# All modulation rows on TensorE, in four column groups of the array, and none left for attention

## The chip, the cores and the metric

The kernel runs on one core of a Trainium2 chip. The core has TensorE (matmuls, shown as PE, its weight loads as PEld), VectorE (DVE), ScalarE (ACT), GpSimd (POOL) and SyncE (SP), which here only issues transfers. Each engine takes its instructions in the order in which they were written for it, and engines wait for each other by semaphores. The metric is the time of one execution on the device, in microseconds (us).

## The reference, cut to what matters

One layer of a diffusion backbone over 512 latent and 256 context tokens of width 1024. The conditioning vector `c` gives six modulation vectors for the latent tokens, and the learned vector `c_ctx` gives those of the context tokens; all that is computed from them here is

```python
mod  = (silu(c) @ w_mod + b_mod).reshape(B, 6, D)        # w_mod: 1024 x 6144
modc = (silu(c_ctx) @ w_mod + b_mod).reshape(6, D)       # only shift and scale 0, 1 are used
h  = modulate(rmsnorm(x, norm_mix), mod[0], mod[1])      # h * (1 + scale) + shift
hc = modulate(rmsnorm(ctx, norm_mix), modc[0], modc[1])
p  = h @ w_in + b_in                                     # q, kv, rope key, Hyena input, gates
attn = attention(q, keys and values of context and latent)
hy   = hyena(...)                                        # long convolutions by FFT
x = x + mod[2] * merge_branches(attn, hy, gates)
h2 = modulate(rmsnorm(x, norm_ffn), mod[3], mod[4])
x = x + mod[5] * moe(h2)                                 # 64 experts, top 8, and a shared one
return rmsnorm(x, final_norm)
```

So `mod` is a product of one vector (two vectors for the first two parts) with a matrix of 1024 x 6144 fp32 numbers, 25 MB.

## The kernel before, in words

The matrix `w_mod` is cut into 24 column blocks of 256; a block is 1024 x 256, that is 8 pieces of the contraction with 128 rows each. Blocks 0 to 7 (shift and scale of the first norm) are needed at once and are computed in the **prologue**, by `mod_rows` (line 196): eight fp32 matmuls per block, with the two columns of `c2` (silu of `c` and of `c_ctx`) as the stationary side and the weight piece `wm` as the moving side, into the PSUM tile `pm`. ScalarE copies the two rows out (`row`), two transposes (`ptm`, line 205) turn them into columns, VectorE adds the bias into `sh`. `sh` feeds `stream`, which makes the modulated, transposed tokens `hT` and `hTc`. While this runs, the Hyena filters (`filt`) use the same engines.

Blocks 8 to 23 are needed only after attention, as rows in the DRAM tensor `modd`. Before the change, twelve of them (`NM = 12`) are computed by `mod_later` (line 481) between the projections of the **Hyena and gate stage** (`conv_block`, `long_conv`, `gate`): SP loads four `wn` tiles of 256 KB per block into three buffers; ScalarE multiplies each piece by its 128 numbers of silu(`c`) (lines 489, 493) and GpSimd adds the pieces up in `ac` (line 494), or, in every third block at first, VectorE does both in one instruction (line 491). One matmul with a column of ones (`pn`, line 498) then sums over the partitions, VectorE adds the bias row `br`, and GpSimd writes the row to `modd`. `br` has one buffer, and the PSUM tag `ms` of `pn` has one bank. The last four blocks are computed in **attention** by `mod_last` (line 792), with GpSimd for products and sums and the tiles `mb0`, `mb1`, and finished by two matmuls `pnl` (line 837).

The program is written stage by stage, but it is not run in that order: a scheduler sets the order of each engine's instructions before the run, from priorities and its own estimates, so that work of a later line can stand ahead of an earlier one. On each engine that order is then fixed. Attention's first matmuls are those of the keys (`pkn`), the values (`pv`) and the queries (`pq`); the gate matmuls are `pg`, and the Hyena inverse transform is `py`, which reads the table `tit`. Nearly all transfers from DRAM are issued by SP, in order, one queue for all of them.

Of the kernel before, what the change touches and what calls it, by code (L numbers as in the profile page):

```python
# [11 lines left out]
F32 = mybir.dt.float32  # L12
# [9 lines left out]
D = 1024  # L22
# [29 lines left out]
def kernel(ctx: ExitStack, tc: tile.TileContext, x, ctxt, wmod, bmod, win, wuq, wuk, wuv, wba, wbh,  # L52
# [73 lines left out]
    def v(col, n=1, p=128):  # L126
        return vec[:p, col:col + n]
# [15 lines left out]

    scb = const.tile([128, 8], F32, name="scb")
    cb2 = const.tile([128, 12], F32, name="cb2")
# [28 lines left out]
    sp.dma_start(w2t, fw2)  # L174
    sc = mp.tile([128, 16], F32, name="sc")
    act.activation(sc, v(V_C, 16), AF.Silu)
    wmt = {}
    order = [0, 4, 1, 5, 2, 6, 3, 7]
    xs = {"l": [], "c": []}

    def mod_load(q):
# [9 lines left out]

    c2 = mp.tile([128, 8, 2], F32, name="c2")
    dve.tensor_copy(c2[:, :, 0], sc[:, 0:8])
    dve.tensor_copy(c2[:, :, 1], sc[:, 8:16])
    sh = mp.tile([128, 16, 2], F32, name="sh")

    def mod_rows(q):
        pm = bank(f"pm{q}", 256, "pm")
        for j in range(8):
            mm(pm[:2], c2[:, j, :], wmt[q][j // 4][:, j % 4, :], j == 0, j == 7)  # L200
        row = mp.tile([2, 256], F32, name=f"row{q}", tag="row")
        act.copy(row, pm[:2])
        pt = bank(f"ptm{q}", 4, "ms")
        for i in range(2):
            pe.transpose(pt[:, 2 * i:2 * i + 2], row[:, i * 128:(i + 1) * 128], ident[:2, :2])
        dve.tensor_tensor(sh[:, 2 * q:2 * q + 2, :], pt.rearrange("p (i c) -> p i c", c=2),
                          v(V_BM + 2 * q, 2).unsqueeze(2).to_broadcast([128, 2, 2]), ALU.add)
# [50 lines left out]
    for q in range(4):  # L258
# [3 lines left out]
        split(w3p[q // 2][:, q % 2, 0], w3p[q // 2][:, q % 2, 1], xq, lo_eng=gp)  # L262
    sp.dma_start(tit, ti)
    rl1 = fp.tile([128, 2, 4], F32, name="rl1")
# [98 lines left out]
    for i, q in enumerate(order):  # L363
        if i >= 2:
            mod_rows(q)
            if i + 3 < 8:
                mod_load(order[i + 3])
        if i % 2 == 1:
            js = slice(i - 1, i + 1)
            dve.tensor_scalar(A[:, js], sh[:, 8 + i - 1:8 + i + 1, :], 1.0, None, ALU.add)  # L370
            dve.tensor_tensor(A[:, js], A[:, js], v(V_NM + i - 1, 2).unsqueeze(2).to_broadcast([128, 2, 2]), ALU.mult)
            for j in range(i - 1, i + 1):
                stream(j, "l", 0, hT)
                stream(j, "c", 1, hTc)
    mst.close()
    p1st.close()
# [101 lines left out]
    m2p = m2.enter_context(tc.tile_pool(name="m2p", bufs=1, reuse_waits="tile"))  # L478
    act.activation(scb, v(V_C, 8), AF.Silu)

    def mod_later(q, on_dve):

        ac = m2p.tile([128, 256], F32, name=f"ac{q}", tag="ac", bufs=2)
        for j in range(8):
            if j % 2 == 0:
                wq = m2p.tile([128, 2, 256], F32, name=f"wn{q}{j}", tag="wn", bufs=3)
                sp.dma_start(wq, wmod[8 + q, :, j:j + 2, :])
            if j == 0:
                act.mul(ac, wq[:, 0], scb[:, j:j + 1])
            elif on_dve:  # L490
                dve.scalar_tensor_tensor(ac, wq[:, j % 2], scb[:, j:j + 1], ac, ALU.mult, ALU.add)
            else:
                act.mul(wq[:, j % 2], wq[:, j % 2], scb[:, j:j + 1])  # L493
                gp.tensor_tensor(ac, ac, wq[:, j % 2], ALU.add)  # L494
        br = m2p.tile([1, 256], F32, name=f"br{q}", tag="br", bufs=1)
        sp.dma_start(br, bmod[:, q * 256:(q + 1) * 256])
        pm = bank(f"pn{q}", 256, "ms")
        mm(pm[:1], ones[:, 0:1], ac)
        dve.tensor_tensor(br, br, pm[:1], ALU.add)
        gp.dma_start(modd[:, q * 256:(q + 1) * 256], br)  # L500

    def conv_block(i):

        ps, = proj(i, f"hy{i}")
        raw = up.tile([128, T], F32, name=f"raw{i}", tag="raw", bufs=2)
        act.activation(raw, ps, AF.Identity, bias=v(V_BIN + i))
        d = up.tile([128, T], F32, name=f"u{i}", tag="u", bufs=12)
        act.activation(d, ps, AF.Identity, bias=cb2[:, i:i + 1], scale=v(V_CW + 12 + i))
        w0, w2 = v(V_CW + i), v(V_CW + 24 + i)
        dve.scalar_tensor_tensor(d[:, 128:512], raw[:, 0:384], w0, d[:, 128:512], ALU.mult, ALU.add)  # L510
        dve.scalar_tensor_tensor(d[:, 1:128], raw[:, 384:511], w0, d[:, 1:128], ALU.mult, ALU.add)
        dve.scalar_tensor_tensor(d[:, 0:384], raw[:, 128:512], w2, d[:, 0:384], ALU.mult, ALU.add)
        dve.scalar_tensor_tensor(d[:, 384:511], raw[:, 1:128], w2, d[:, 384:511], ALU.mult, ALU.add)
        mod_later(chunk[0], chunk[0] % 3 == 2)
        chunk[0] += 1
        return d
# [78 lines left out]
    chunk = [0]  # L595
    NM = 12
    LATE = 5
# [26 lines left out]
    for i in range(16 - LATE):  # L624
        gate(i)
        if chunk[0] < NM:
            mod_later(chunk[0], False)
            chunk[0] += 1
# [85 lines left out]
    xt = [modp.tile([128, D], F32, name=f"xt{a}", tag=f"xt{a}") for a in range(NA)]  # L714
    mb = [modp.tile([128, D], F32, name=f"mb{i}", tag=f"mb{i}") for i in range(2)]
    hyst = ExitStack()
# [74 lines left out]

    def mod_last(i):

        k, j2 = divmod(i, 4)
        ac = mb[1][:, k * 256:(k + 1) * 256]
        wq = mb[0][:, i % 2 * 512:i % 2 * 512 + 512].rearrange("p (j c) -> p j c", j=2)
        tc.keep_in_program_order(sp.dma_start(wq, wmod[8 + NM + k, :, 2 * j2:2 * j2 + 2, :]))
        tc.keep_in_program_order(gp.tensor_tensor(
            wq, wq, scb[:, 2 * j2:2 * j2 + 2].unsqueeze(2).to_broadcast([128, 2, 256]), ALU.mult))
        if j2 == 0:  # L800
            gp.tensor_tensor(ac, wq[:, 0], wq[:, 1], ALU.add)
        else:
            for j in range(2):
                gp.tensor_tensor(ac, ac, wq[:, j], ALU.add)

    for u in range(2 * H + 2):
# [6 lines left out]
        if 7 <= u < 11:  # L813
# [4 lines left out]
            gp.tensor_tensor(hyT[kt][:, 1], raw, hyT[kt][:, 0].bitcast(F32), ALU.subtract)  # L818
        if 2 <= u < 10:
            mod_last(2 * u - 4)  # L820
            mod_last(2 * u - 3)
        if u % 2 == 0 and u // 2 + 1 < H:
# [7 lines left out]
        if u >= 2:  # L830
            mix(u - 2)
    row = mb[0][0:1]
    sp.dma_start(row, bmod[:, NM * 256:])
    for n in range(2):
        cs = slice(n * 512, (n + 1) * 512)
        pm = bank(f"pnl{n}", tag="pq")
        mm(pm[:1], ones[:, 0:1], mb[1][:, cs])
        dve.tensor_tensor(row[:, cs], row[:, cs], pm[:1], ALU.add)
    gp.dma_start(modd[:, NM * 256:], row)
    ast.close()  # L840
# [700 lines left out]
```

## Time and profile before

| | |
|---|---|
| time, median of 3 runs | 1391.62 us (1391.15 to 1392.55) |
| the profiled execution's own time | 1393.19 us |
| its span | 1391.4 us |
| TensorE busy | 1285.2 us, 92% of the span |
| VectorE, ScalarE, GpSimd busy | 1143.1, 902.6, 427.0 us |
| granted TensorE clock, mean | 0.972 of 2.4 GHz |
| data moved | 332.79 MB |

The span is what the hardware profiler saw of the one profiled execution, from its first to its last instruction; the execution's own time is 1.8 us longer. Busy times of different engines overlap. A matmul is pipelined, so the sum of single durations is more than the time that TensorE was busy; shares are of the union. Every fp32 matmul appears as two instructions. The mixture of experts takes the time from about 600 us to the end, and the change has no instruction in it.

### The profile page before, as it was taken

Reading aid. Unit: us, or ns where it says so; the run is one execution under the profiler, and the core shown is the slowest. Engines: PE = TensorE matmul, PEld = TensorE weight load, DVE = VectorE, ACT = ScalarE, POOL = GpSimd, SP = SyncE. Lnnn points to the kernel's source line nnn. Section 1 sums busy time; section 2 is a strip of 40 time slices with the busy share of each in tenths; the row PEclk is TensorE's granted clock in tenths of the full one; section 3 lists DMA queues with packets and bytes.
Section 4 is the critical chain, followed back from the end, with each engine's and each line's share of the span. In section 5 each row is a group of like instructions: output and inputs, shape, how many; then the busy total and the mean of one; then the engine's idle time right before and its main releaser. Section 6 shows DMA issues by size and latency. Waiting matters only on the chain.

```text
span 1391.4 us, 19516 instructions
## 1 busy us (share of the span) xinstructions
PE 1285.2 (92%) x6758; PEld 1045.1 (75%) x6758; DVE 1143.1 (82%) x1735; ACT 902.6 (65%) x1366; POOL 427.0 (31%) x341
## 2 busy tenths in 40 slices
PE   6999998887999998899999999999999999999970
PEld 2476886666888786778888888888888888888750
DVE  5879899788788647778988988889888888889855
ACT  4556553443777436546787877778788787777851
POOL 2433146756576256441112111211111111111120
PEclk8999999998999999999999999999999999999995
DMA  9444345454233556467999999899999999999944
GB/s 330 172 137 147 113 153 168 158 172 155 87 105 102 187 170 224 164 268 269 324 319 330 319 317 316 275 325 314 318 323 312 322 327 333 296 313 293 320 111 179
DMA packets 83875, 332.79 MB, mean 239 GB/s; under 512 B 14433, under 2 KB 15981, under 8 KB 56383
## 3 DMA queue, kind: packets, MB, share of 16 engines
q1 hardware_dynamic: 70366, 305.19, 61.3%
q0 software_dynamic: 11104, 22.14, 8.3%
q10 hardware_dynamic: 2304, 4.20, 0.8%
q8 instruction: 53, 0.87, 0.2%
q14 instruction: 48, 0.39, 0.1%
HBM read 296.91 MB, written 52.97 MB: 251 GB/s over the span
## 4 chain that ended last, share of the span: by engine, by line
PE 68%; DVE 10%; DMA 10%; issue 5%; POOL 3%; ACT 3%; SPq 0%; POOLq 0%; DVEq 0%; ACTq 0%
PE pge L100 8%; PE pge L99 8%; PE pge L101 8%; PE pxe L1158 4%; PE pxe L1159 4%; PE pye L101 4%; PE pye L99 4%; PE pye L100 4%; DMA accd<-Ye,ixe 4%; DMA wn<-in_wmod_dram 3%; POOL ac L494 2%; DMA accd<-Ys,ixs 1%; PE phy L101 1%; PE phy L99 1%; PE phy L100 1%
## 5 line engine op out<-in xcount | busy, mean ns | idle before, releaser
L1019 POOL DMA_INDIRECT accd<-Ye,ixe x64 | 111.8, 1747 | 601.2 <-ACT Ye L1018 306.6
L1158 PE MATMUL pxe<-oge,h2h 128*128 128x256 f32 x512 | 131.2, 289 | 0.3
L1159 PE MATMUL pxe<-oge,h2l 128*128 128x256 f32 x512 | 126.9, 280 | 0.0
L1158 PEld LDWEIGHTS pxe<-oge,h2h 128*128 128x128 f32 x512 | 96.4, 188 | 3.7 <-issue 0.6
L1159 PEld LDWEIGHTS pxe<-oge,h2l 128*128 128x128 f32 x512 | 96.4, 188 | 3.1
L494 POOL TENSOR_TENSOR ac<-ac,wn 128x256 f32<-128x256 f32 x56 | 67.0, 1196 | 46.8 <-ACT wn L493 32.3
L1018 ACT COPY Ye<-pye 128x1024 f32<-128x1024 f32 x64 | 65.0, 1016 | 7.6 <-PE pye L101 6.1
L991 ACT ACTIVATE aae<-pge 128x256 f32<-128x256 f32 x64 | 24.7, 386 | 32.5 <-PE pge L101 32.5
L493 ACT ACTIVATE wn<-wn,scb 128x256 f32<-128x256 f32 x56 | 25.6, 501 | 30.6 <-DMA wn<-in_wmod_dram 29.8
L92 PE MATMUL pm<-wm,c 128*2 128x256 f32 x128 | 35.1, 428 | 0.8 <-DMA wm<-in_wmod_dram 0.8
L753 PE MATMUL pT<-ident,P 128*128 128x128 f32 x192 | 31.2, 277 | 4.9 <-DVE PT41l L106 1.5
L1139 DVE TENSOR_TENSOR oge<-iot,posm 128x256 fp32r<-128x256 f32 x64 | 23.7, 418 | 13.2 <-PE pxe L1159 13.2
L732 DVE TENSOR_REDUCE st<-S 128x1 f32<-128x768 f32 x32 | 30.3, 948 | 1.3 <-PE S L101 1.1
L992 DVE SCALAR_TENSOR_TENSOR aae<-aae,wge,pge 128x256 f32<-128x256 f32 x64 | 30.5, 476 | 0.7
L734 ACT ACTIVATE P<-S,st 128x768 f32<-128x768 f32 x32 | 29.1, 910 | 1.8 <-DVE st L732 1.4
L293 POOL TENSOR_TENSOR ab<-ab,f 128x256 f32<-128x256 f32 x12 | 10.7, 892 | 61.8 <-DVE f L292 35.9
L753 PEld LDWEIGHTS pT<-ident,P 128*128 128x128 f32 x192 | 21.9, 140 | 9.2 <-DVE PT41l L106 1.8
L92 PEld LDWEIGHTS pm<-wm,c 128*2 128x2 f32 x128 | 10.8, 92 | 20.9 <-issue 10.1
L92 PEld LDWEIGHTS sle<-R,oge 128*64 128x64 f32 x256 | 23.1, 137 | 4.2
L95 PE MATMUL pte<-ident,aae 128*128 128x128 f32 x128 | 24.4, 272 | 0.0
L92 PE MATMUL sle<-R,oge 128*64 128x4 f32 x256 | 23.1, 189 | 0.0
L95 PEld LDWEIGHTS pte<-ident,aae 128*128 128x128 f32 x128 | 17.6, 140 | 7.3
(7025 smaller groups left out, 4955.2 us busy)
## 6 DMA issues: line engine op xcount, KB each, us to landing
gu0e<-in_wgu_dram SPq DMA_DIRECT2D x64, 1024.0 KB, 7.4
gu1e<-in_wgu_dram SPq DMA_DIRECT2D x64, 1024.0 KB, 7.2
de<-in_wd_dram SPq DMA_DIRECT2D x64, 1024.0 KB, 6.8
wn<-in_wmod_dram SPq DMA_DIRECT2D x48, 256.0 KB, 3.2
wm<-in_wmod_dram SPq DMA_DIRECT2D x16, 512.0 KB, 8.0
rg<-in_win_dram SPq DMA_DIRECT2D x32, 256.0 KB, 2.9
rwo<-in_wout_dram SPq DMA_DIRECT2D x32, 256.0 KB, 3.1
rhy<-in_win_dram SPq DMA_DIRECT2D x24, 256.0 KB, 2.9
```

Of the source, the lines that this page charges most:

```text
L92: pin(pe.matmul(o, lhsT, rhs, start=start, stop=stop))
L95: pin(pe.transpose(o, i, idn))
L99: pe.matmul(o, lt[0], rt[0], start=start, stop=False)
L100: pe.matmul(o, lt[0], rt[1], start=False, stop=False)
L101: pe.matmul(o, lt[1], rt[0], start=False, stop=stop)
L494: gp.tensor_tensor(ac, ac, wq[:, j % 2], ALU.add)
L753: pe.transpose(pT[:, i * 128:(i + 1) * 128], P[:, kt * 128:(kt + 1) * 128], ident)
L992: dve.scalar_tensor_tensor(self.aa, self.aa, self.wg, pg[:, FF:], ALU.mult, ALU.mult)
L1018: act.copy(Y, py)
L1019: gp.indirect_dma_start(out=accd, out_offset=bass.IndirectOffsetOnAxis(ap=self.ix, axis=0), in_=Y, in_offset=None, compute_op=ALU.add, bou ...
L1158: pe.matmul(o, h2h[:, a, js], oh, start=(a % 2 == 0), stop=False)
L1159: pe.matmul(o, h2l[a][:, js], oh, start=False, stop=(a % 2 == 1))
```

## The change

All 24 blocks go to TensorE. `mod_parts` puts the eight pieces of a block's contraction in turn into four column groups of the array: piece j goes to output partitions 32 (j mod 4) and up, with a stationary side `sc32` of 32 columns, of which the first holds silu(`c`), the second silu(`c_ctx`) and the rest zeros. The output tile then holds four partial sums in partitions 0, 32, 64 and 96. One more matmul per row or turn with `cols32` (ones at those four partitions) adds the four up. `mod_later` now makes all of blocks 8 to 23 (`NM = 16`), and `mod_last`, `pnl`, the tiles `mb` and the sums on ScalarE, GpSimd and VectorE are gone. In the prologue the copied-out rows are put in `tit`, whose own load moves behind the last of them.

```diff
-    scb = const.tile([128, 8], F32, name="scb")
+    sc32 = const.tile([128, 8, 32], F32, name="sc32")
+    gp.memset(sc32, 0.0)
+    cols32 = const.tile([128, 32], F32, name="cols32")
+    dve.tensor_reduce(cols32, ident.rearrange("p (g c) -> p c g", g=4), AX.X, ALU.add)
...
-    sc = mp.tile([128, 16], F32, name="sc")
-    act.activation(sc, v(V_C, 16), AF.Silu)
+    for i in range(2):
+        act.activation(sc32[:, :, i], v(V_C + 8 * i, 8), AF.Silu)
...
+    def mod_parts(pm, w):
+
+
+        for j in range(8):
+            g = 32 * (j % 4)
+            mm(pm[g:g + 32], sc32[:, j], w(j), j < 4, j >= 4)
...
     def mod_rows(q):
         pm = bank(f"pm{q}", 256, "pm")
-        for j in range(8):
-            mm(pm[:2], c2[:, j, :], wmt[q][j // 4][:, j % 4, :], j == 0, j == 7)
-        row = mp.tile([2, 256], F32, name=f"row{q}", tag="row")
-        act.copy(row, pm[:2])
+        mod_parts(pm, lambda j: wmt[q][j // 4][:, j % 4, :])
+
+        row = tit[:, q % 4].rearrange("p r c -> p (r c)")
+        act.copy(row, pm)
         pt = bank(f"ptm{q}", 4, "ms")
         for i in range(2):
-            pe.transpose(pt[:, 2 * i:2 * i + 2], row[:, i * 128:(i + 1) * 128], ident[:2, :2])
+            mm(pt[:, 2 * i:2 * i + 2], row[:, i * 128:(i + 1) * 128], cols32[:, 0:2])
...
-    sp.dma_start(tit, ti)
     rl1 = fp.tile([128, 2, 4], F32, name="rl1")
...
                 stream(j, "c", 1, hTc)
+    sp.dma_start(tit, ti)
...
-    def mod_later(q, on_dve):
-
-        ac = m2p.tile([128, 256], F32, name=f"ac{q}", tag="ac", bufs=2)
-        for j in range(8):
-            if j % 2 == 0:
-                wq = m2p.tile([128, 2, 256], F32, name=f"wn{q}{j}", tag="wn", bufs=3)
-                sp.dma_start(wq, wmod[8 + q, :, j:j + 2, :])
-            if j == 0:
-                act.mul(ac, wq[:, 0], scb[:, j:j + 1])
-            elif on_dve:
-                dve.scalar_tensor_tensor(ac, wq[:, j % 2], scb[:, j:j + 1], ac, ALU.mult, ALU.add)
-            else:
-                act.mul(wq[:, j % 2], wq[:, j % 2], scb[:, j:j + 1])
-                gp.tensor_tensor(ac, ac, wq[:, j % 2], ALU.add)
+    def mod_later(q):
+
+        wq = []
+        for h in range(4):
+            wq.append(m2p.tile([128, 2, 256], F32, name=f"wn{q}{h}", tag="wn", bufs=3))
+            sp.dma_start(wq[h], wmod[8 + q, :, 2 * h:2 * h + 2, :])
         br = m2p.tile([1, 256], F32, name=f"br{q}", tag="br", bufs=1)
         sp.dma_start(br, bmod[:, q * 256:(q + 1) * 256])
-        pm = bank(f"pn{q}", 256, "ms")
-        mm(pm[:1], ones[:, 0:1], ac)
-        dve.tensor_tensor(br, br, pm[:1], ALU.add)
+        pm = bank(f"pn{q}", tag="ms")
+        mod_parts(pm[:, 0:256], lambda j: wq[j // 2][:, j % 2])
+        ac = m2p.tile([128, 256], F32, name=f"ac{q}", tag="ac")
+        act.copy(ac, pm[:, 0:256])
+        mm(pm[:1, 256:512], cols32[:, 0:1], ac)
+        dve.tensor_tensor(br, br, pm[:1, 256:512], ALU.add)
         gp.dma_start(modd[:, q * 256:(q + 1) * 256], br)
...
-        mod_later(chunk[0], chunk[0] % 3 == 2)
+        mod_later(chunk[0])
...
-    NM = 12
+    NM = 16
...
-    def mod_last(i):
...
-        if 2 <= u < 10:
-            mod_last(2 * u - 4)
-            mod_last(2 * u - 3)
...
-    row = mb[0][0:1]
-    sp.dma_start(row, bmod[:, NM * 256:])
-    for n in range(2):
-        cs = slice(n * 512, (n + 1) * 512)
-        pm = bank(f"pnl{n}", tag="pq")
-        mm(pm[:1], ones[:, 0:1], mb[1][:, cs])
-        dve.tensor_tensor(row[:, cs], row[:, cs], pm[:1], ALU.add)
-    gp.dma_start(modd[:, NM * 256:], row)
```

The scheduler gives the changed program another order; three places of it follow. The number behind `pn`, `wn` and `br` is that of the block (0 to 15, counted from block 8 of the matrix), and for `wn` a second one is that of its tile; `x2` and `x4` are so many equal instructions.

TensorE, where the last but one block's matmul stands before, among the gate matmuls:

```order
L101 MATMUL pg11512_3191<-hTh_83,wg111l_3213 128x512
L92 MATMUL pn10_2163<-ac10_2137,ones_72 1x256
L101 MATMUL pg12512_3231<-hTh_83,wg120l_3235 128x512
L99 MATMUL pg12512_3231<-hTh_83,wg120h_3234 128x512
L100 MATMUL pg12512_3231<-hTl_84,wg120h_3234 128x512
```

One matmul of modulation stands there between gate matmuls, as do the eleven others; 48 gate matmuls stand even behind attention's first matmul (`pkn`), among those of its keys, values and queries.

TensorE in the changed program, at the end of the gate matmuls (`pg15` is the last gate):

```order
L92 MATMUL pn7_1892<-wn73_1888,sc32_76 32x256 x2
L99 MATMUL pg15512_3394<-hTh_86,wg151h_3415 128x512
L100 MATMUL pg15512_3394<-hTl_87,wg151h_3415 128x512
L101 MATMUL pg15512_3394<-hTh_86,wg151l_3416 128x512
L92 MATMUL pn7_1892<-ac7_1901,cols32_78 1x256
L92 MATMUL pn8_1961<-wn80_1951,sc32_76 32x256 x2
L92 MATMUL pn8_1961<-wn81_1953,sc32_76 32x256 x2
L92 MATMUL pn8_1961<-wn82_1955,sc32_76 32x256 x2
L92 MATMUL pn8_1961<-wn83_1957,sc32_76 32x256 x2
L92 MATMUL pn8_1961<-ac8_1970,cols32_78 1x256
L92 MATMUL pn9_2030<-wn90_2020,sc32_76 32x256 x2
L92 MATMUL pn9_2030<-wn91_2022,sc32_76 32x256 x2
```

Blocks 0 to 7 are spread over the stage, as blocks 0 to 11 were; blocks 8 to 15 moved to its end, one after the other in the way that `pn8` is shown, with no other matmul between, and attention's first matmul (`pkn`) follows the last of them.

SP's queue in the changed program at the same place:

```order
L493 DMA wn90_2020<-in_wmod_dram 128x512
L493 DMA wn91_2022<-in_wmod_dram 128x512
L495 DMA br8_1959<-in_bmod_dram 1x256
L493 DMA wn92_2024<-in_wmod_dram 128x512
L493 DMA wn93_2026<-in_wmod_dram 128x512
L493 DMA wn100_2089<-in_wmod_dram 128x512
L495 DMA br9_2028<-in_bmod_dram 1x256
L493 DMA wn101_2091<-in_wmod_dram 128x512
```

Before, loads of gate weights (`rg`) stand between those of `wn` and `br` up to the end. Now the last nine `br` and the `wn` between them follow each other, each `wn` behind the use of the tile three places ahead of it and each `br` behind the write of the one before; attention's weights (`rwq`, `rwuv`) come after all of them.

## Rows read from the trace of the kernel before

**Rows 1.** The page: busy time by engine; the chain by engine.

```profile
PE 1285.2 (92%) x6758; PEld 1045.1 (75%) x6758; DVE 1143.1 (82%) x1735; ACT 902.6 (65%) x1366; POOL 427.0 (31%) x341
...
PE 68%; DVE 10%; DMA 10%; issue 5%; POOL 3%; ACT 3%; SPq 0%; POOLq 0%; DVEq 0%; ACTq 0%
```

**Rows 2.** Windows: length, then PE, PEld, DVE, ACT, POOL busy; clock; DMA; GB/s.

```profile
35.00:79.40 44.40, 39.50 (x214) 22.61 (x213) 38.52 (x80) 24.90 (x49) 21.58 (x20) 0.96 0.42 156
...
185.00:341.00 156.00, 131.65 (x657) 102.36 (x656) 134.93 (x194) 63.72 (x123) 101.76 (x76) 0.95 0.49 160
341.00:470.00 129.00, 122.41 (x764) 105.08 (x762) 105.77 (x213) 93.49 (x199) 72.47 (x87) 1.00 0.31 107
```

**Rows 3.** Waits of PE, 85 to 340 us: total, times, longest.

```profile
PE pg L101 <- POOL wg50l L106: 6.3, 1, 6.3
PE pg L101 <- POOL wg111l L106: 5.1, 1, 5.1
```

**Rows 4.** Groups by line, 85 to 340 us: busy, mean ns, idle before.

```profile
L494 POOL TENSOR_TENSOR ac<-ac,wn 128x256 f32<-128x256 f32 x56 | 67.0, 1196 | 46.8 <-ACT wn L493 32.3 <-ACT ac L489 12.1
L493 ACT ACTIVATE wn<-wn,scb 128x256 f32<-128x256 f32 x56 | 25.6, 501 | 30.6 <-DMA wn<-in_wmod_dram 29.8 <-DVE u L512 0.6
L491 DVE SCALAR_TENSOR_TENSOR ac<-wn,scb,ac 128x256 f32<-128x256 f32 x28 | 16.8, 602 | 4.1 <-DMA wn<-in_wmod_dram 3.9
...
L92 PE MATMUL pn<-ac,ones 128*1 128x256 f32 x24 | 7.2, 380 | 0.8 <-DVE br L499 0.8
...
L489 ACT ACTIVATE ac<-wn,scb 128x256 f32<-128x256 f32 x12 | 6.1, 506 | 24.0 <-DMA wn<-in_wmod_dram 17.0 <-PE pg L100 6.5 <-PE pn L92 0.6
...
L92 PE MATMUL pl<-ones,ab 128*128 128x1 f32 x16 | 2.1, 235 | 0.5 <-DVE rl L327 0.5
```

**Rows 5.** Waits of SP's queue, 85 to 340 us.

```profile
SPq L487 <- POOL ac L494: 64.9, 32, 8.3
SPq L496 <- DMA modd<-br: 21.0, 10, 4.7
```

**Rows 6.** Timeline of PE in the prologue: start, duration.

```profile
58.40 0.28 PE L205 MATMUL ptm<-ident,row 2*128 2x2 f32 x2
58.61 3.62 PE L92 MATMUL pm<-wm,c 128*2 128x256 f32 x16
```

**Rows 7.** Windows of the instructions on `pm` alone: PE, PEld, ACT.

```profile
40.50:70.50 30.00, 17.81 (x72) 5.43 (x72) 1.75 (x5) 0.94 0.35 120
```

**Rows 8.** Groups by line on POOL, 341 to 470 us.

```profile
L804 POOL TENSOR_TENSOR mb<-mb,mb 128x256 f32<-128x256 f32 x24 | 17.7, 736 | 1.3
L798 POOL TENSOR_TENSOR mb<-mb,scb 128x512 f32<-128x512 f32 x16 | 16.8, 1050 | 6.3 <-DMA mb<-in_wmod_dram 6.3
```

**Rows 9.** Tile `wn`, 85 to 345 us: its loads, from issue.

```profile
DMA to landing us min/median/max: 2.9/3.2/4.1
```

**Rows 10.** Timelines of ACT, PE and POOL where work is handed over.

```profile
19.03 0.36 ACT L202 COPY row<-pm 2x256 f32<-2x256 f32 x1
...
19.44 0.28 PE L205 MATMUL ptm<-ident,row 2*128 2x2 f32 x2 [2.00 <-ACT row L202]
...
184.67 0.62 ACT L105 CAST why101h<-rhy 128x512 fp32r<-128x512 f32 x1 [0.86 <-PE phy L100]
...
338.00 0.59 PE L92 MATMUL pn<-ac,ones 128*1 128x256 f32 x2
...
339.76 0.50 POOL L500 DMA_DIRECT2D modd<-br  x1 [0.69 <-DVE br L499]
```

**Rows 11.** The chain that ended last, 205 to 222 us: start, duration.

```profile
214.16 3.39 DMA modd<-br
...
217.56 1.71 DMA br<-in_bmod_dram
```

**Rows 12.** Windows of 7 us around the idle time before `wg111l`.

```profile
315.00:322.00 7.00, 1.39 (x4) 0.60 (x4) 6.16 (x7) 2.12 (x4) 6.92 (x4) 0.72 0.02 9
322.00:329.00 7.00, 5.37 (x13) 3.46 (x14) 3.96 (x7) 1.64 (x3) 3.95 (x6) 0.55 0.79 247
```

More of the change, by code (lines that the diff above doesn't have):

```diff
@@ L190, in x_load @@
             xs[nm].append(xi)
-    c2 = mp.tile([128, 8, 2], F32, name="c2")
-    dve.tensor_copy(c2[:, :, 0], sc[:, 0:8])
-    dve.tensor_copy(c2[:, :, 1], sc[:, 8:16])
     sh = mp.tile([128, 16, 2], F32, name="sh")
@@ L478 @@
     m2p = m2.enter_context(tc.tile_pool(name="m2p", bufs=1, reuse_waits="tile"))
-    act.activation(scb, v(V_C, 8), AF.Silu)
-    def mod_later(q, on_dve):
-        ac = m2p.tile([128, 256], F32, name=f"ac{q}", tag="ac", bufs=2)
-        for j in range(8):
-            if j % 2 == 0:
-                wq = m2p.tile([128, 2, 256], F32, name=f"wn{q}{j}", tag="wn", bufs=3)
-                sp.dma_start(wq, wmod[8 + q, :, j:j + 2, :])
-            if j == 0:
-                act.mul(ac, wq[:, 0], scb[:, j:j + 1])
-            elif on_dve:
-                dve.scalar_tensor_tensor(ac, wq[:, j % 2], scb[:, j:j + 1], ac, ALU.mult, ALU.add)
-            else:
-                act.mul(wq[:, j % 2], wq[:, j % 2], scb[:, j:j + 1])
-                gp.tensor_tensor(ac, ac, wq[:, j % 2], ALU.add)
+    def mod_later(q):
[3 more added lines that the diff above has]
+            sp.dma_start(wq[h], wmod[8 + q, :, 2 * h:2 * h + 2, :])
         br = m2p.tile([1, 256], F32, name=f"br{q}", tag="br", bufs=1)
         sp.dma_start(br, bmod[:, q * 256:(q + 1) * 256])
-        pm = bank(f"pn{q}", 256, "ms")
-        mm(pm[:1], ones[:, 0:1], ac)
-        dve.tensor_tensor(br, br, pm[:1], ALU.add)
+        pm = bank(f"pn{q}", tag="ms")
[4 more added lines that the diff above has]
+        dve.tensor_tensor(br, br, pm[:1, 256:512], ALU.add)
         gp.dma_start(modd[:, q * 256:(q + 1) * 256], br)
@@ L626 @@
         if chunk[0] < NM:
-            mod_later(chunk[0], False)
+            mod_later(chunk[0])
             chunk[0] += 1
@@ L714 @@
     xt = [modp.tile([128, D], F32, name=f"xt{a}", tag=f"xt{a}") for a in range(NA)]
-    mb = [modp.tile([128, D], F32, name=f"mb{i}", tag=f"mb{i}") for i in range(2)]
     hyst = ExitStack()
@@ L790, in route_prep @@
                     R[:, a, :, c], iot[:, 130:131].to_broadcast([128, NE]), float(a - NONE), 1.0 - c, ALU.add, ALU.mult))
-    def mod_last(i):
[L794 to L804, printed above, removed]
     for u in range(2 * H + 2):
```

## The prediction

> **What bounds the kernel now.** I read the page first, for what is scarce: TensorE is busy 92% of the span, and 68% of the chain that ended last is its work [rows 1]. Then the busy times by stage, because the change only touches the first 470 us [rows 2]. In every stage up to there TensorE is the fullest engine or next to it, and what it leaves idle is small: 4.9 us from 35 to 79.4, 24.4 us (156.00 less 131.65) from 185 to 341, 6.6 us from 341 to 470. VectorE comes second and is nearly full too in the second stage (38.52 of 44.40 us). So time comes from two places only: TensorE work that goes away or is added, and idle time of TensorE that goes away or is added.
>
> Why it is idle from 185 to 341 is in the lists of waits. TensorE's longest ones are for low halves of gate weights that GpSimd makes: 6.3 and 5.1 us lead the list [rows 3]. GpSimd is late because it carries the modulation sums: 56 additions, 67.0 us [rows 4]. The DMA queue of SP is held by the same sums, 64.9 us in all, because a weight tile is free only when its sum is done, and 21.0 us by the single buffer `br` [rows 5]. Modulation there costs TensorE itself almost nothing: twelve `pn` matmuls, 7.2 us [rows 4].
>
> **The change, part by part.** *The matmuls in column groups.* Eight matmuls of one block take 3.62 us today, shown as 16 instructions, so 0.226 us each: every fp32 matmul is two instructions [rows 6]. After the change the block's matmuls go to groups 0, 1, 2, 3, 0, 1, 2, 3. No row shows two column groups at work at once, so I bound it: no overlap, 3.62 us; four at once, 0.9 us. I take a value between. The two instructions of one matmul belong to the same group and stand next to each other, and TensorE starts matmuls in order, so the second waits for the first and only it can run beside the next group's first. Sixteen instructions then take nine slots of 0.226 us, 2.04 us.
>
> The Trainium skill, "TensorE: Matmul & The Clock Gate", section "Part 3: Packing small matmuls — row/col tiling", says that small matmuls in distinct column groups run concurrently in the same array, and gives 2.38x for three groups. No row here shows it. By that figure a block takes about 1.5 us, an estimate, and the sum below would be about 5 us lower.
>
> *Prologue (35 to 79.4 us).* From 40.5 to 70.5 the old matmuls hold TensorE for 17.81 us [rows 7]. Nine slots for sixteen leave 10.0, so 7.8 us go. The two turns of a row, 0.28 us a block today [rows 6], become two full fp32 matmuls; the nearest row is `pl`, eight matmuls in 2.1 us, so about 0.28 us each [rows 4]: 0.28 us more a block, 1.3 us over the four and a half blocks (72 of 16 instructions each) of this stretch. Net 6.5. But VectorE's 38.52 us cannot be passed, so at most 44.4 - 38.5 = 5.9 us are to be had. I take **-5** (0 or slightly worse without overlap, -5.9 at best). The memset, the small reduction and the two Silu run while the first weights are still on their way. The load of `tit` is now behind the last row on SP's queue; behind it stand `H` and small tables, and `tit` is first read by `py`, more than 100 us later. I cost it at nothing; if it were late, `py` would wait for one load.
>
> *First eight blocks of the later part.* They stand between projection and gate matmuls as the old `pn` did. TensorE gets 8 x (2.04 + 0.60) = 21.1 us more and loses the old twelve `pn` (7.2) and the two `pnl` of attention, each twice as wide as a `pn` of 0.60, so some 2.4 [rows 4]: **+11.5** (+2.4 with four at once, +24.2 with no overlap).
>
> *What the relief gives.* GpSimd's 67.0 us, 31.7 us of ScalarE, 16.8 us of VectorE go [rows 4], replaced by sixteen ScalarE copies of about 0.36 us. GpSimd's halves are then on time, and weight tiles are freed by TensorE itself. I let 17 of the 24.4 us of idle go, since some waits are for VectorE and ScalarE (bounds 0 and 24). In attention GpSimd loses 34.5 us in two kinds of steps [rows 8], but TensorE is idle there for 6.6 us only [rows 2], of which I let 2.5 go. Together **-19.5**.
>
> *Last eight blocks.* This decides. The rows of the changed order show the last eight blocks in one piece on TensorE, 73 matmuls with nothing between, after the last gate matmul and ahead of attention's first. TensorE works in order, so whatever a block waits for, TensorE waits for. One block's loop, from the end of one bias addition to the next: the matmuls start when VectorE has freed the only `ms` bank. There are three `wn` buffers and four tiles a block, so the load of the fourth tile starts when the first is used up. The terms:
> - two matmuls on the first tile, three slots: 0.7 us;
> - the load of the fourth tile: 3.2 us, 2.9 to 4.1 [rows 9] (the two tiles between are worked off under it);
> - two matmuls on the fourth tile: 0.7 us;
> - ScalarE's copy: from its start to the next matmul 19.03 to 19.44, with the hand-over 0.5 us [rows 10];
> - the last matmul, the addition and the hand-over: 338.00 to 339.76, 1.76 us [rows 10].
>
> That is 6.9 us. The other loop, through `br`, is shorter: the write of `modd` 3.39, the load of `br` 1.71 [rows 11], and 1.2 from the last matmul's end over the addition to the next engine (the 1.76 above less 0.59) make 6.3 us, so it hides under the first. TensorE is busy 38% of such a loop. Where it had stood idle for long, the granted clock was 0.72 and 0.55 over 7 us, while it was 0.95 over the whole stage [rows 2, 12], a mix of its two levels 2.4 and 1.2 GHz. At the lower level all through, the three matmul terms double: 8.9 us. I take the middle, 7.9 us, times 8: **+63** (55 to 71).
>
> *After it.* Attention's weights stand behind all this on SP's queue. Before, 48 gate matmuls lay among attention's first matmuls and filled such waits; now they are ahead of the block. A load of their size (3.2 us [rows 9]) and the two steps that split it (0.62 us on ScalarE [rows 10], VectorE's taken alike) are 4.4 us, and the keys, values and queries come after each other: **+5** (0 to 10).
>
> Sum: -5 + 11.5 - 19.5 + 63 + 5 = +55.0 us. The profiled execution took 1393.19 us (span 1391.40 and 1.79 around it), 1.6 us above the median of the runs, 1391.62. So 1448.2 on its scale, 1446.6, say 1447, on the median's.
>
> **The rivals.** *No overlap at all*: prologue +1.3 instead of -5, the first eight blocks +24.2, the tail's loop 0.45 longer: 1470. For it: the rows show none. Against: the instructions address different groups.
> *Four at once*: prologue -5.9, first eight blocks +2.4, loop 0.5 shorter: 1433. For it: the four groups write to different partitions and share nothing but their input rows. Against it: the two instructions of one fp32 matmul share a group. (The section of the Trainium skill named above describes this case; no row here shows it.)
> *TensorE waits for the loads in the first eight blocks too*: wherever ScalarE waited for a `wn` load (29.8 us over 56 [rows 4]), TensorE would now wait, and none of the 19.5 us is won: 1466. Against it: in the new order 23 or more matmuls (over 5 us at 0.226 us) lie between the block's third and fourth tile, more than a load.
> *The tail does not wait (the other side)*: if the eight blocks took only TensorE's own time, the tail would cost 21 us instead of 63 and the kernel 1405. With four groups at once they would take 1.5 us each, and the kernel 1386, faster than before. It decides from a loop of 2.2 us with four at once (1433 less 8 x 5.2 us), 1.0 us otherwise. For it: tiles that land early. Against it: three buffers, one bank and a 3.2 us load in a closed loop.
>
> **How the numbers follow.** Forecast 0.58, no overlap 0.15, four at once 0.15, loads late everywhere 0.09, tail without waits 0.03. A measurement of this kernel can tell about 0.2%, 3 us. Faster 0.03; within 0.2% 0.02, from ends of the cases between; slower 0.95. The forecast's own range is 1436 to 1458 from the clock and the load; the neighbours widen it to 1420 to 1472.
>
> **What would show it.** In the changed profile: a stretch of some 63 us ahead of attention in which TensorE is under half busy and waits for `wn` loads, ScalarE's `ac` and VectorE's `br` in turn, eight times; `pm` blocks of about 2 us where they took 3.62; GpSimd's gate halves no longer among TensorE's waits; from 470 us of the old time on nothing but a shift. I am wrong if the blocks in the tail follow each other at 3 us or less, or if `pm` blocks still take 3.6 us or under 1.

## The result, and the profile after

The changed kernel takes 1440.1 us (median of 5 runs, 1438.76 to 1450.46) against 1391.62 us: ratio 1.0345, 95% interval 1.0324 to 1.0366. The forecast was 1447 us, within 1420 to 1472. The profiled execution took 1450.46 us, 10 us over the median. In it the mixture of experts, which the change doesn't touch, took 5.3 us longer than before (780.5 against 775.2 us from the first matmul of its tile `pxe` to the end, 772.6 to 777.0 in all experiments but one); where the rest was lost, one profile doesn't show. So mainly its first 410 us are read here.

One instant tells nearly all: the start of attention's first `S` matmul. From there to the end of the span the kernel before takes 1391.4 - 362.2 = 1029.2 us, and the kernels of the experiments 1023 to 1038. These are the rows of tile `S` (last columns: first and last start), of before and of after:

```profile
L99 PE MATMUL S<-KT00h,Q0h x8: 277/338/501, 362.2 to 369.3; 128*128 128x512 f32 x4, 128*128 128x256 f32 x4
```
```profile
L99 PE MATMUL S<-KT00h,Q0h x8: 274/338/506, 409.8 to 420.9; 128*128 128x512 f32 x4, 128*128 128x256 f32 x4
```

It starts 47.6 us later, which is nearly the whole result of 48.5. Where in these 410 us, the windows show (columns as in [rows 2]). After, cut at the first projection, at the first block of the last piece, at attention's first matmul `pkn` and at `S`:

```profile
79.89:335.80 255.91, 252.57 (x1328) 199.59 (x1326) 192.58 (x316) 103.12 (x175) 57.88 (x42) 0.99 0.45 143
335.80:397.27 61.47, 31.93 (x144) 5.18 (x144) 3.69 (x10) 4.67 (x11) 3.91 (x8) 0.55 0.44 139
397.27:409.80 12.53, 10.84 (x33) 8.52 (x34) 7.65 (x12) 6.49 (x15) 3.65 (x5) 0.63 0.54 194
```

Before, cut at the same events (there `pkn` follows the last modulation matmul without a piece between):

```profile
79.36:343.70 264.34, 236.68 (x1164) 188.87 (x1163) 227.23 (x355) 125.98 (x234) 125.96 (x103) 0.95 0.46 151
343.70:362.20 18.50, 18.50 (x85) 15.60 (x84) 8.42 (x13) 10.82 (x23) 7.49 (x7) 1.00 0.32 106
```

The first stage got 8.4 us shorter although it holds 48 gate matmuls more, and TensorE's idle time in it fell from 27.7 to 3.3 us. Then come 61.5 us that did not exist. Their timeline on TensorE (start, duration, in brackets the idle time before and what ended it):

```profile
336.27 0.64 PE L92 MATMUL pn<-wn,sc 128*32 128x256 f32 x8 [0.50 <-DVE br L501]
337.47 0.62 PE L92 MATMUL pn<-wn,sc 128*32 128x256 f32 x4 [0.56 <-DMA wn<-in_wmod_dram]
340.35 0.62 PE L92 MATMUL pn<-wn,sc 128*32 128x256 f32 x4 [2.25 <-DMA wn<-in_wmod_dram]
341.44 0.85 PE L92 MATMUL pn<-ac,cols 128*1 128x256 f32 x2 [0.47 <-ACT ac L499]
342.80 1.08 PE L92 MATMUL pn<-wn,sc 128*32 128x256 f32 x8 [0.50 <-DVE br L501]
...
374.04 2.03 PE L92 MATMUL pn<-wn,sc 128*32 128x256 f32 x12 [0.50 <-DVE br L501]
379.12 1.07 PE L92 MATMUL pn<-wn,sc 128*32 128x256 f32 x4 [3.06 <-DMA wn<-in_wmod_dram]
380.72 1.01 PE L92 MATMUL pn<-ac,cols 128*1 128x256 f32 x2 [0.53 <-ACT ac L499]
382.23 2.15 PE L92 MATMUL pn<-wn,sc 128*32 128x256 f32 x12 [0.50 <-DVE br L501]
...
397.27 0.69 PE L99 MATMUL pkn<-kvnh,wukh 128*128 128x384 f32 x1 [0.50 <-DVE br L501]
```

The first block takes 6.5 us, most of it at the full clock. From the second on the clock is at its lower level (granted 0.50 from 342.8 us to `pkn`): four instructions last 1.07 instead of 0.62 us, and a block 7.4 to 8.3. Each block waits for its fourth tile (the first two for another tile as well), once for ScalarE and once for VectorE. The sums of these waits from 336 to 398 us (total, times, longest):

```profile
PE pn L92 <- DMA wn<-in_wmod_dram: 20.9, 10, 3.2
PE pn L92 <- ACT ac L499: 4.2, 8, 0.5
PE pn L92 <- DVE br L501: 4.0, 8, 0.5
```

And the list that answers to [rows 3], from 185 to 336 us, complete; of GpSimd's late halves 0.9 us is left:

```profile
PE pg L101 <- POOL wg10l L106: 0.9, 1, 0.9
PE pn L92 <- DMA wn<-in_wmod_dram: 0.5, 1, 0.5
```

In the prologue the same sixteen instructions that took 3.62 us [rows 6] now take 1.07 at the full clock, and 2.27 earlier on:

```profile
8.35 2.27 PE L92 MATMUL pm<-wm,sc 128*32 128x256 f32 x16 [1.26 <-DMA wm<-in_wmod_dram]
...
47.93 1.07 PE L92 MATMUL pm<-wm,sc 128*32 128x256 f32 x16
```

The clock before 44.8 us has to be read from the durations: the windows give 1.00 for it, but up to there the matmuls last about as long as at 0.50 in the piece (eight instructions of `pm` 1.08 us at 41.30, 0.64 at 44.81; eight of `pn` 1.08 at 342.80). From 61.7 to 72 us the windows themselves give 0.50.

And yet the first projection starts at 79.89 us, where it was 79.36. In the window of [rows 2] TensorE fell from 39.50 to 33.26 us, and VectorE rose from 38.52 to 42.79:

```profile
35.00:79.40 44.40, 33.26 (x226) 23.95 (x225) 42.79 (x93) 28.42 (x54) 21.58 (x21) 0.88 0.48 171
```

By the durations, about 20 of these 44.4 us were at the lower clock; the row before, at 0.96, has less than 4.

### The profile page after: what moved, and what is told of

Its sections match the earlier page's. It is cut to its first block, busy times and chain, and to the rows that moved or that the text cites. A ratio compares the mean times of both kernels' runs of the same rounds, so it can differ in the third digit from the quotient of the medians.

```text
span 1448.6 us, 19866 instructions
## 1 busy us (share of the span) xinstructions
PE 1313.4 (91%) x7034; PEld 1058.9 (73%) x7034; DVE 1116.7 (77%) x1708; ACT 882.3 (61%) x1314; POOL 331.2 (23%) x245
## 5 line engine op out<-in xcount | busy, mean ns | idle before, releaser
L995 POOL DMA_INDIRECT accd<-Ye,ixe x64 | 116.0, 1813 | 601.8 <-ACT Ye L994 238.0
L501 DVE TENSOR_TENSOR br<-br,pn 1x256 f32<-1x256 f32 x16 | 6.5, 406 | 74.6 <-PE pn L92 74.6
L92 PE MATMUL pn<-wn,sc 128*32 128x256 f32 x256 | 37.4, 496 | 25.4 <-DMA wn<-in_wmod_dram 21.4
L499 ACT COPY ac<-pn 128x256 f32<-128x256 f32 x16 | 6.0, 373 | 72.3 <-PE pn L92 72.3
L92 PEld LDWEIGHTS pn<-wn,sc 128*32 128x32 f32 x256 | 8.8, 122 | 51.2 <-DMA wn<-in_wmod_dram 34.6
L1115 DVE TENSOR_TENSOR oge<-iot,posm 128x256 fp32r<-128x256 f32 x64 | 23.8, 420 | 13.4 <-PE pxe L1135 13.3
L300 POOL TENSOR_TENSOR ab<-ab,f 128x256 f32<-128x256 f32 x12 | 9.4, 785 | 89.9 <-DVE ab L297 44.8
L502 POOL DMA_DIRECT2D modd<-br x16 | 8.0, 502 | 82.7 <-DVE br L501 74.8
```

Source lines behind the costliest of these rows:

```text
L92: pin(pe.matmul(o, lhsT, rhs, start=start, stop=stop))
L995: gp.indirect_dma_start(out=accd, out_offset=bass.IndirectOffsetOnAxis(ap=self.ix, axis=0), in_=Y, in_offset=None, compute_op=ALU.add, bou ...
```

## Experiments

Each kernel starts from the changed one unless said otherwise; `S` is its first start. Ratios are to the kernel before on the same chip.

**1. Another bank for the sums.** Theory: the piece is the loss. Rivals: TensorE's own work for the blocks, or attention's start.

```diff
-        pm = bank(f"pn{q}", tag="ms")
+        pm = bank(f"pn{q}", tag="pj")
```

> The changed kernel with one word altered: the sums of blocks 8 to 23 (tile pn) go to the three banks of tag pj, which the projections use, instead of the single bank ms. In the written order ms first serves the last filter sums (pl), so that pn of block 0 could not start before them. Theory (the loss is the piece of eight blocks at the end, each closing a loop over buffers, and the column groups themselves are a gain): the blocks start earlier, spread among the projections, no piece is left before attention; 62.1 us go, the eight blocks' own TensorE work of 1.6 us each comes back: 1440.1 - 62.1 + 13 = 1391 us (1383 to 1397). Rival (the added matmuls of TensorE, or the switching between column groups, cost the time): it stays above 1420 us wherever the blocks stand. Rival (attention's start is what was lost): no piece, but attention's first S as late as now, above 1420 us too.

1408.44 us, ratio 1.0097 (1.0066 to 1.0128), `S` at 382.7. No piece is left: the first `pn` starts at 117.5 us instead of 183.7. So 27 us of the 47.6 up to `S` went with the piece, but 17 us more than the theory's 1391 remain. The trace has them: `pn` keeps TensorE busy for 39.1 us where 13 were reckoned for the eight blocks and as much for the rest, since a block now comes in parts of six, two and one matmuls, in which fewer groups meet; and `pn` waits for loads, and for its bank until a gate's sigmoid has read it:

```profile
PE pn L92 <- DMA wn<-in_wmod_dram: 7.4, 6, 1.7
PE pn L92 <- ACT sg L623: 6.5, 1, 6.5
```

The measured 1408 lies between the theory and its rivals. That the bank decides the place was not in the prediction. Tiles of one bank are handed out in the written order, and `ms` first serves the filters' `pl`. Before, only a block's last matmul needed the bank, and the sums ran ahead of it on other engines; now the whole contraction does, and its weight tiles stay occupied until then.

The Trainium skill, "Perfetto Trace Analysis", section "Matmuls", advises to let independent groups of matmuls rotate through different banks, so that one is emptied while the next is filled. Here three banks instead of one brought `S` 27 us forward, and the waits of `pn` for VectorE's `br` fell from 4.0 to 0.6 us; so most of it came from the blocks' earlier place and not from such an overlap.

**2. Two buffers for `br`.** Which of the two loops sets a block's time?

```diff
-        br = m2p.tile([1, 256], F32, name=f"br{q}", tag="br", bufs=1)
+        br = fp.tile([1, 256], F32, name=f"br{q}", tag="ab", bufs=2)
```

> The changed kernel with two buffers for the bias row br instead of one; nothing else. The piece at the end stays, with nine blocks instead of eight. Theory (the loop through the load of the fourth wn tile sets a block's time, the loop through br hides under it): blocks still follow each other every 7.5 to 8 us, the ninth adds one more: 1440 to 1449 us. Rival (the loop through br sets it): blocks follow at about 5 us, 1415 to 1428 us.

1441.78 us, ratio 1.0323 (1.0264 to 1.0383); nine blocks, which still follow each other every 7.1 to 7.9 us. The loop is that of the fourth tile:

```profile
342.74 2.06 PE L92 MATMUL pn<-wn,sc 128*32 128x256 f32 x12 [0.50 <-DVE br L501]
346.77 1.07 PE L92 MATMUL pn<-wn,sc 128*32 128x256 f32 x4 [1.98 <-DMA wn<-in_wmod_dram]
348.37 1.01 PE L92 MATMUL pn<-ac,cols 128*1 128x256 f32 x2 [0.53 <-ACT ac L499]
349.88 2.02 PE L92 MATMUL pn<-wn,sc 128*32 128x256 f32 x12 [0.50 <-DVE br L501]
```

**3. Five buffers for `wn` too.** With a block and a tile ahead, does the load leave the loop? `br` has two buffers as in 2.

```diff
+            late = (4 * q + h) % 5 > 2
-            wq.append(m2p.tile([128, 2, 256], F32, name=f"wn{q}{h}", tag="wn", bufs=3))
+            wq.append((fp if late else m2p).tile([128, 2, 256], F32, name=f"wn{q}{h}", tag="slo" if late else "wn",
+                                                 bufs=2 if late else 3))
...
```

> The changed kernel with five buffers for the weight tiles wn instead of three (two of them in memory that the filters leave free) and two for br; the bank stays ms. Five blocks are left in the piece at the end. Theory: with a whole block loaded ahead no load stands in the loop; what is left at the lower clock is 2.25 us of matmuls, 0.53 to ScalarE's copy, 1.0 for the sum and 0.5 to VectorE's addition, 4.3 us a block, 21 us in all, and the three blocks that moved forward cost 1.6 us each: 1440.1 - 62.1 + 21 + 5 = 1404 us (1396 to 1412). Rival (the piece costs by its place and its blocks, the bank alone, 7.7 us a block): 5 x 7.7 = 39 us, 1422 us.

1399.3 us, ratio 1.0027 (1.0002 to 1.0051), `S` at 371.1. Five blocks are left in the piece, 21.0 us. That is 4.2 each where 4.3 were reckoned, but the reckoning was for the lower clock and the granted clock is 1.00, so the match is in part luck; what is left of load waits is 0.2 to 1.4 us:

```profile
328.29 0.59 PE L92 MATMUL pn<-ac,cols 128*1 128x256 f32 x2 [0.57 <-ACT ac L501]
329.38 0.62 PE L92 MATMUL pn<-wn,sc 128*32 128x256 f32 x4 [0.50 <-DVE br L503]
331.37 0.62 PE L92 MATMUL pn<-wn,sc 128*32 128x256 f32 x4 [1.37 <-DMA wn<-in_wmod_dram]
332.26 1.29 PE L92 MATMUL pn<-wn,sc 128*32 128x256 f32 x8 [0.27 <-DMA wn<-in_wmod_dram]
334.07 0.59 PE L92 MATMUL pn<-ac,cols 128*1 128x256 f32 x2 [0.53 <-ACT ac L501]
```

So three buffers (two for `wn`, one for `br`, which did nothing by itself) undo 38.7 of the 47.6 us, with the bank as it was.

**4. No column groups.** What is the packing worth?

```diff
-            g = 32 * (j % 4)
-            mm(pm[g:g + 32], sc32[:, j], w(j), j < 4, j >= 4)
+            mm(pm[0:32], sc32[:, j], w(j), j == 0, j == 7)
...
```

The copies and the sums read these 32 partitions alone.

> The changed kernel without column groups: all eight pieces of a block go to output partitions 0 to 31 and add up there, and the copies and sums read these alone. Number and size of the matmuls are the same. Theory (four groups run at once): a block's sixteen instructions take 3.6 us instead of 1.07; the blocks among the gate matmuls cost 2.5 us more each (8 x 2.5 = 20), those of the piece about 1 us more, and the prologue 0 to 6 us, since VectorE is full there: 1440.1 + 20 + 7 + 3 = 1470 us (1455 to 1480). Rival (groups overlap little, and a block is short because of its 32 columns of weights): 1437 to 1443 us.

1450.18 us, ratio 1.0387 (1.0332 to 1.0442). Sixteen instructions take 3.64 us, as [rows 6] had it, but the kernel does not lose 30 us to the changed one: by the ratios (1.0345 there) it is 6 us, with overlapping intervals, and by `S`, now at 420.5, 10.7. Theory and rival both missed. The first projection comes 0.9 us later, and the piece does not grow. Its last seven blocks without groups, and the last seven of the changed kernel:

```profile
357.85:409.16 51.31, 37.19 (x126) 13.21 (x126) 2.88 (x8) 3.62 (x9) 3.39 (x7) 0.87 0.44 139
```
```profile
342.80:397.27 54.47, 29.19 (x126) 4.65 (x126) 2.88 (x8) 4.12 (x9) 3.39 (x7) 0.50 0.42 132
```

The slower matmuls run under the load. TensorE is busier with them (37.2 of 51.3 us against 29.2 of 54.5), its granted clock is 0.87 against 0.50, and a block takes 7.3 us against 7.8. What was lost was lost ahead of them, for the most part among the gate matmuls: from the first projection to these seven blocks it takes 277.1 us, the changed kernel 262.9.

**5. The prologue alone.** The kernel before, with only blocks 0 to 7 in column groups (the edits of the change to `mod_rows`).

> The kernel before with the prologue alone changed: blocks 0 to 7 in four column groups, the rest (blocks 8 to 23 by ScalarE, GpSimd and VectorE, four of them in attention) as it was. Theory: TensorE's work there falls by some 17 us, but VectorE is busy 43.4 of 45 us from 35 to 80 us in the changed kernel, so the first projection (pkv) stays at 79 to 81 us and the time is that of before: ratio 0.997 to 1.003. Rival (the saved TensorE time is the kernel's, as the term of -5 us had it, and was lost later in the changed kernel): pkv at 74 us, ratio 0.996 or less.

1394.08 us, ratio 1.0028 (1.0009 to 1.0048). The first projection starts at 78.2 us, and the window shows why no more:

```profile
35.00:79.40 44.40, 33.32 (x226) 24.05 (x223) 43.56 (x89) 27.20 (x50) 23.04 (x22) 0.92 0.47 169
```

VectorE is busy 43.56 of 44.40 us. The term of -5 was not there to be had: the projection came 1.2 us earlier, and the kernel gained nothing.

**6. Bank, `wn` and `br` together.** The edits of 1, 2 and 3.

> The changed kernel with all three edits: pn in the three banks of the projections, five wn buffers, two for br. All sixteen blocks then stand among other matmuls, each with its eight pieces in one go. Theory: TensorE's 25 us for pn against 7 before the change remain, some 20 us of its idle time between 80 us and attention's first S go, and attention has 3 us less to do: 1390 to 1397 us, ratio 0.998 to 1.003, so no gain over before is left to be had by placing. Rival (the relief of GpSimd is worth more than TensorE's work, once no wait is left): 1380 us or less, ratio under 0.993.

1395.12 us, ratio 1.0016 (0.9999 to 1.0033). From 80 us to `S` TensorE is busy for 278 us and idle for 14, nearly the same as in experiment 3 (278 and 13), though no piece is left: the idle time now lies among the filters, where the blocks moved. No kernel here with all sixteen blocks on TensorE came below the kernel before.

**7. Four blocks on TensorE, four on GpSimd, four on VectorE.** Blocks 1, 4, 7, 10 as in the changed kernel, the others and attention as before, buffers and banks of experiment 6.

```diff
...
     def mod_later(q, on_dve):
+        if q % 3 == 1:
+            return mod_pe(q)
...
```

`mod_pe` is `mod_later` as the change has it.

> A mixture: the prologue in column groups; of the twelve blocks of the later stage four (1, 4, 7, 10) on TensorE in column groups, four on ScalarE and GpSimd and four on VectorE as before, pn in the banks of the projections, five wn and two br buffers; the last four blocks in attention as before. Theory (TensorE's work is the price, GpSimd's lateness the gain): the four blocks cost 1.1 to 1.4 us each over one pn matmul, 5 us, and GpSimd's 34 us of additions that go take its 14.2 us of waits of TensorE away: 1391.6 + 5 - 14 = 1382 us, ratio 0.989 to 0.997. Rival (GpSimd's waits are replaced by others, or the gate matmuls that now stand in attention cost as much): 1.000 or more.

1428.75 us, ratio 1.0269 (1.0241 to 1.0297), a miss. GpSimd's waits went, but other and larger ones came:

```profile
PE pn L92 <- DVE ac L518: 15.4, 4, 9.7
PE pz L557 <- DVE u L617: 5.0, 2, 4.8
PE fpb L99 <- ACT sd102h L105: 4.5, 1, 4.5
PE za L100 <- DVE zT010l L106: 4.3, 1, 4.3
```

The other bank lets the blocks start among the filters, and VectorE's own blocks with them; TensorE meets a `pn` whose sum VectorE has not finished.

**8. Neighbours in one group.** Does TensorE start a block's instructions strictly in order?

```diff
-            g = 32 * (j % 4)
-            mm(pm[g:g + 32], sc32[:, j], w(j), j < 4, j >= 4)
+            g = 32 * (j // 2)
+            mm(pm[g:g + 32], sc32[:, j], w(j), j % 2 == 0, j % 2 == 1)
```

> The changed kernel with another order of column groups: the pieces go to groups 0, 0, 1, 1, 2, 2, 3, 3 instead of 0, 1, 2, 3, 0, 1, 2, 3, so that four instructions of one group follow each other. If a group's instructions wait only for their own group and others pass them by, a block still takes 1.07 us and the time is 1436 to 1444. If TensorE starts instructions in order, as the nine slots of the prediction had it, only the three changes of group overlap: thirteen slots of 0.226, 2.9 us a block (those in one go in the prologue show it), 8 x 1.9 = 15 us more for the blocks among the gates and 0 to 1 us each in the piece: 1455 to 1463.

1470.62 us, ratio 1.0569 (1.0541 to 1.0597). At the granted clock 1.00 a whole block takes 1.09 us, as with the groups in turn (1.07), and not 2.9; half a block, which is now four instructions in each of two groups, takes 1.06:

```profile
42.85 1.71 PE L92 MATMUL pm<-wm,sc 128*32 128x256 f32 x16
...
45.67 1.06 PE L92 MATMUL pm<-wm,sc 128*32 128x256 f32 x8
...
52.35 1.09 PE L92 MATMUL pm<-wm,sc 128*32 128x256 f32 x16
```

The first of these blocks ran while the clock rose (granted 0.61 over its 1.71 us, 0.50 before it) and says nothing of the order. Four instructions in one group take 1.05 us by themselves (experiment 4), so in the half block the second group ran wholly beside the first, and in the whole block all four did. Their instructions did pass waiting ones: that each engine takes its instructions in the order written, as the first section has it, does not hold between column groups.

So the first theory had TensorE right, but neither had the time. The kernel lost 30 us: `S` comes 26.8 us later than in the changed kernel, 5 of them from the prologue and 21 from the piece. It has nine blocks instead of eight, each 9.2 us instead of 7.7. At the lower clock the last four instructions of a block, now all in one group, take up to 1.92 us instead of 1.07, and the twelve before them up to 2.9 instead of about 2.05.

**9. Twelve blocks.** The kernel of experiment 3 with `NM = 12`; blocks 20 to 23 go back to GpSimd in attention (`mod_last` and `pnl`, as before).

> The kernel with five wn and two br buffers (bank ms), with twelve blocks on TensorE instead of sixteen; the last four go back to GpSimd in attention, as before the change. One block is left in the piece ahead of attention. Theory (each block in that piece costs 4.2 us, and attention hides the four blocks on GpSimd for 3 us): 1399.3 - 4 x 4.2 + 3 = 1385.5 us, ratio 0.990 to 0.997, faster than before. Rival (TensorE's work for the blocks eats all that the relief of GpSimd gives, wherever they stand): 1.000 or more.

1374.96 us, ratio 0.9873 (0.9849 to 0.9898): faster than both kernels. `S` starts at 347.5; one block is left ahead of attention:

```profile
80.00:347.50 267.50, 261.94 (x1432) 205.91 (x1431) 203.38 (x334) 112.81 (x197) 65.03 (x52) 0.99 0.46 153
347.50:1372.90 1025.40, 962.83 (x5221) 810.00 (x5219) 847.82 (x1241) 723.40 (x1036) 261.79 (x201) 0.98 0.79 265
```

From 80 us to `S` TensorE is idle for 5.6 us, and the rest takes 1025.4 us, no more than with attention free of modulation (1026.4 in experiment 3). The gain is 10 us larger than expected: the piece shrank from 21.0 to 2.7 us and began 3.8 us earlier. Whether the kernel before would gain from the additional buffers alone, with its sums on GpSimd and VectorE, was not tried, and neither were twelve blocks without column groups.

**10. and 11. Casts from VectorE to ScalarE.** In `stream`, once with experiment 9 and once with the kernel before.

```diff
-        split(dst[0][:, j], dst[1][:, j], t, hi_eng=dve, lo_eng=gp)
+        split(dst[0][:, j], dst[1][:, j], t, lo_eng=gp)
```

> As the kernel with twelve blocks, and the casts of the high halves of hT and hTc in the prologue go from VectorE to ScalarE (some 9 us of VectorE's 43 in the stretch from 35 to 80 us). Theory (VectorE bounds the prologue once the column groups have relieved TensorE): the first projection starts 3 to 6 us earlier, at 74 to 77 us, ratio 0.003 below that of twelve blocks. Rival (the prologue hangs on the loads of wm, for which TensorE waits 6.5 us, or on the chain of turns and casts): it stays at 79 to 81 us.

> The kernel before with only those casts moved from VectorE to ScalarE. Theory (there TensorE, busy 39.5 of 44.4 us, and VectorE, 38.5, bound the prologue together, so relieving one gives little): first projection at 78 to 80 us, ratio 0.998 to 1.001. Rival (the casts alone are the gain, with or without column groups): 74 to 77 us, ratio 0.997 or less.

With twelve blocks 1383.18 us, ratio 0.9933 (0.9909 to 0.9956); the first projection starts at 76.5 us instead of 78.8, VectorE is down to 38.24 us in the window, and the gain of 2.3 us is lost again behind it: `S` starts at 354.0 instead of 347.5. A new wait of TensorE for GpSimd's `wg90l`, 4.3 us, is the largest part of that; the rest is left open. Alone 1392.97 us, ratio 0.9998 (0.9982 to 1.0015). So VectorE was one bound of the prologue but not the only one.

**12. The mixture of experiment 7, bank `ms`.**

> The mixture of four blocks on TensorE, four on GpSimd and four on VectorE again, with pn in the bank ms instead of the projections' banks, which puts the blocks where they stood before the change, behind the filters. Theory (the mixture lost because the early blocks put VectorE's sums among the filters, where VectorE was late already: TensorE waited 15.4 us for its ac): that wait goes, GpSimd's waits go as well, a piece of one block is left: 1391.6 + 6 - 14 + 3 = 1387 us, ratio 0.992 to 1.000. Rival (the mixture of three methods itself keeps TensorE waiting): over 1.010.

1404.13 us, ratio 1.0086 (1.0060 to 1.0113), a miss again. TensorE still waits 8.2 us for VectorE's `ac`. The profiled execution, 1393 us, was the fastest of seven; what the slower ones did, its trace can't show, and it stays open.

## Why the prediction was right, and where its steps were not

The sign and the cause held: the last eight blocks stand in one piece, TensorE waits in it, and that is the loss. Experiments 1, 3 and 9 take it away or shorten it in three ways, and `S` starts 27, 39 and 62 us earlier (the last with four blocks fewer).

- **Tail**: forecast +63, measured 61.5, with the loop that was named: load of the fourth tile, ScalarE, VectorE (shown by 2 and 3). TensorE was busy for 52% of it, a little more than the half that was named as the sign. The size was right by luck, two errors that cancel. The matmul terms were too large, since four groups run at once, and the clock was at the lower level in seven blocks of eight, where a middle was taken.
- **After it**: +5; measured, `pkn` to `S` takes 12.5 us against 18.5 with 48 gate matmuls of 0.226 us (10.85), so +4.9. The cost does not end there: from `S` to the first `pxe`, early in the mixture of experts, the changed kernel takes 258.3 us against 254.0, and the kernels of 4 and 8, whose attention starts in the same way, 257.7 and 258.1. The forecast that nothing but a shift follows was wrong by these 4 us.
- **Relief**: 17 us of idle time were let go in this stage, 24.4 went (27.7 to 3.3), the bound of 24. Behind `S`, 2.5 us and two `pnl` were to go; by the medians nothing did on balance (48.5 against 47.6 up to `S`).
- **First eight blocks**: the step that failed is "TensorE starts matmuls in order, so the second waits for the first". Nine slots of 0.226 us were forecast, four were used: 1.07 against 2.04 us a block where it comes in one go. The term was hardly off all the same: the blocks come in parts, and up to the piece `pn` costs 18.2 us, not the 13.4 of eight blocks in one go, 11.0 more than the old twelve; less the 2.4 of `pnl`, that is +8.6 against +11.5. The rival "four at once" had the mechanism; its 1433 falls short because it also took the whole prologue gain.
- **Prologue**: -5 forecast, +0.5 measured, the lower bound "0 or slightly worse" for another reason than given there. TensorE's work fell as reckoned (6.2 us in the window), but VectorE's was taken as fixed at 38.5 us and is 42.8: 2 us that ran before 35 us came in later (20.10 there before, 18.08 now), and single steps got longer (the casts of `hTch` 698 ns instead of 447), for a reason that no run shows. TensorE's steps got longer as well where the clock was lower, about 20 us of the window instead of 4. What that cost was not tried; experiment 10 shows only that VectorE was one bound and not the only one.

Up to `S` the measured steps add up to 0.5 + 11.0 - 24.4 + 61.5 + 4.9 = 53.5, and `S` came 47.6 us later. The other matmuls of the first stage account for the difference: the 384 gate matmuls took 93.8 us where 336 took 85.9, 3 us less than with the 10.85 counted for the 48 that moved, at a mean clock of 0.99 instead of 0.95. That the clock is the reason was argued, not tried. So the sum was near by luck, because its terms were off in both directions: prologue +5.5, blocks -2.9, relief -7.4, matmuls around them -5.9, and behind `S` +5.8, the `pnl` among it; with the tail's -1.5 that is the 6.5 us between 55.0 and 48.5.

The Trainium skill, "TensorE: Matmul & The Clock Gate", section "Part 3: Packing small matmuls — row/col tiling", has small matmuls in distinct column groups run concurrently, 2.38x for three; the trace agrees, 3.64 / 1.07 = 3.4x for four.

What failed in experiment 7, and as far as its trace shows in 12, was a step that the sum has too: work was counted by engine, and not by when VectorE could do it.

## What to carry to other kernels

When work moves to an engine that stops at each of its waits, every buffer, bank and queue that it passes becomes that engine's wait: count tiles per unit of work against buffers, and look which earlier user of the bank stands before it in the written order. A faster operation pays only where its engine is the last to finish; here packing gave nothing in the prologue (VectorE was nearly full) nor in the piece (loads), and some 14 us among the gate matmuls (experiment 4), where TensorE is the fullest engine. And engines with slack are worth using: GpSimd did four blocks under attention at no cost that the trace shows, while sixteen blocks keep TensorE busy for 32.3 us even in experiment 3, and twelve on TensorE, with the added buffers, beat both sixteen and the kernel before.

## What the hardware showed that was not expected

- Four column groups overlap fully, also for fp32 matmuls of two instructions each: 1.07 us against 3.64, four slots instead of sixteen.
- A wait-bound stretch got shorter with slower matmuls: seven blocks took 51.3 us unpacked at a granted clock of 0.87, and 54.5 packed at 0.50.
- Instructions of a free group pass those that wait for a busy one: eight in two groups, four after four, took 1.06 us, and sixteen in four groups 1.09, as long as four in one group (1.05).
